# A second mixer's seven-product gate: one product's weight tiles split later, and forms of x made in fewer steps with copies on another queue

## The chip, the core and the metric

The kernel runs on one core of a Trainium2 chip. The core has TensorE (PE, matrix products; its weight loads are listed as PEld), VectorE (DVE), ScalarE (ACT), GpSimd (POOL) and SyncE (SP), each with its own queue of instructions that it works through in order; DMA transfers are issued from such queues, here from those of SP and POOL. Engines wait for one another by semaphores. The metric is the time of one execution in microseconds on the device; lower is better.

## The reference

A decoder trunk of two layers for an input of 512 positions and width 1024, all in fp32. Each layer adds a token mixer and then a gated convolutional feed-forward block, each followed by a layer norm:

```python
for i in range(DEPTH):                       # DEPTH = 2
    y = gla_mixer(...) if i % 3 == 0 else gdn_mixer(...)
    h = layer_norm(ALPHA * h + y, ...)
    h = layer_norm(ALPHA * h + conv_ffn(h, ...), ...)
```

The second mixer, which the change is about, is a gated DeltaNet with 8 heads of 128 and chunks of 64:

```python
proj = x @ w_in
qkv, gate, beta_lin, a_lin = jnp.split(proj, [...])
qkv = silu(causal_dwconv(qkv, conv_w))
o = rms_norm(gdn_chunked(qc, kc, vc, beta, gc), norm_w)
return (o * silu(gate)) @ w_out
```

`gdn_chunked` solves one unit lower triangular system per head and chunk, and then carries a state from chunk to chunk. `gate` is the product of x with a 1024 by 1024 part of `w_in`.

## The kernel before

Every fp32 product is made as three products of rounded halves (fp32r): x is kept as xh + xl, and each weight tile, 128 x 1024 in fp32, is split into wh and wl: ACT casts the tile to wh, DVE subtracts wh from the tile to get wl (`split_out`, L718). TensorE then adds wh·xh, wl·xh and wh·xl in PSUM (`mm`, L214; transposes L232).

The mixers are at 0 to 215 us (gated linear attention) and 565 to 865 us (gated DeltaNet), with the feed-forward blocks behind each.

**The seven products.** The gate's projection is made by `gated` (L1255) from seven products of half the size instead of eight, in the order of GATED: b21, b11, t1, b22, t2, t3, t4. Each has two weight tiles (i = 0 and 2) and a form of x: a quarter of x as it is (a12, a11, a22) or a sum of quarters (w1, v4, v2, v3). The third product t1 takes weights b11 + b12: after the tile of b11 is split, an accumulating DMA on POOL's queue adds the quarter b12 to the same tile in SBUF (L465, tiles `gw`). When that has landed, the tile is split again for t1, and further accumulates follow for later products. In the trace the products are the groups fold<-wh,xh, fold<-wl,xh and fold<-wh,xl; `sg` is the gate that they end in.

**When a tile is split.** `self.look` is how many tiles `prefetch` (L471) splits ahead of the one that TensorE takes; four pairs wh, wl exist (WB). `gated` sets it to 3, and to 2 in the middle of t3. The order in each engine's queue is fixed when the kernel is built, from the order of the program and a planned time for each instruction; on the chip an engine keeps to it, so a split that was planned early stands ahead of what comes behind it, whether its tile has landed or not.

**Forms of x.** `x_forms_within` (L1208) is a generator that runs beside the products: `yield n` hands back until some n us of the planned time have passed, and `until` waits for a mark. It forms w1 first; then `whole` (L1219) fills four tiles `xq` with x's quarters c and d: copies of xh by DMA, and accumulates of xl on top, all on POOL's queue. Sums and differences on DVE (L1176) make v4, v2 and v3 of them, and `put` (L1213) splits each and writes it over a quarter of xh and xl that is no longer needed (L718, xh<-xq and xl<-xq).

**What runs beside.** In the second mixer two more generators feed the engines in the same stretch: `inverses` (L1825) builds the triangular inverses in quarter and half steps (matmuls V and R, copies to T, V and rm on ACT and DVE: L1857 to L1863 for quarters, L1880 and L1883 for halves), and `chain` (L1935) carries the state for two groups of four heads: ks, vn, kT, qs, s, o on TensorE; ACT scales vn (L1960), kd (L1967) and v (L1973), and DVE makes yy (L1952), copies or updates the state (L1980, L1983) and copies o (L1989). vn needs rm, s needs vn and kd, the next ks needs the state. `mixer_out` (L1587) transposes the gated output (yT) and splits it (yh, L1145).

Of the kernel before, what the change touches and what calls it, by code (L numbers as in the profile page):

```python
# [8 lines left out]
F32 = mybir.dt.float32  # L9
# [4 lines left out]
ALU = mybir.AluOpType  # L14
# [63 lines left out]
class Trunk:  # L78
# [1129 lines left out]
    def x_forms_within(self, forms, part, pair, full, both):  # L1208


        nc = self.nc

        def put(name, ts, odd, tok):  # L1213
            for k, t in enumerate(ts):
                self.split_out(part(self.xh, odd, tok, k), part(self.xl, odd, tok, k), pair(t))
            forms[name] = (odd, tok)
            self.set(("form", name), 2.0)

        def whole(odd, tok):  # L1219
            ts = [self.slot("xq") for _ in range(2)]  # L1220
            for x, op in ((self.xh, ALU.bypass), (self.xl, ALU.add)):
                for k, t in enumerate(ts):
                    nc.gpsimd.dma_start(pair(t), part(x, odd, tok, k).bitcast(F32), accum_op=op)
            return ts

        yield from self.until(("rm", 1))
        a = full(0, 256)
        yield 1.5
        b = full(1, 256)
        yield 1.5  # L1230
        both(a, b, ALU.subtract, b)
        yield 2.0
        put("w1", b, 0, 256)
        yield from self.until(("rm", 5))
        c = whole(0, 0)
        d = whole(1, 0)
        yield from self.until(("used", "a11"))
        yield 4.0
        both(c, a, ALU.subtract, a)
        yield 2.0  # L1240
        both(b, c, ALU.subtract, b)
        yield 2.0
        both(b, d, ALU.add, d)
        c = None
        yield 2.0
        put("v4", d, 1, 0)
        d = None
        yield 3.0
        put("v2", b, 0, 0)
        b = None  # L1250
        yield from self.until(("used", "w1"))
        yield 1.0
        put("v3", a, 0, 256)

    def gated(self, forms, tag, done, last):  # L1255


        nc = self.nc
        acc = [[self.psum("fold") for _ in range(2)] for _ in range(2)]
        top, high, right = ([None, None] for _ in range(3))  # L1260

        def operand(form, c, r):
            if isinstance(forms.get(form), tuple):
                odd, tok = forms[form]
                chunk, tok = 2 * c + odd, tok + r * P
                return self.xh[:, chunk, tok:tok + P], self.xl[:, chunk, tok:tok + P]
            if form in forms:
                cols = slice(c % 2 * 256 + r * P, c % 2 * 256 + r * P + P)
                return tuple(t[:, cols] for t in forms[form][c // 2])
            chunk = 2 * c + (form != "a11")  # L1270
            tok = r * P + (256 if form == "a22" else 0)
            return self.xh[:, chunk, tok:tok + P], self.xl[:, chunk, tok:tok + P]

        def copied(ps):
            t = self.slot(tag)
            nc.scalar.copy(t, ps)
            return t

        def update(name, r):
            p, x = acc[0][r], acc[1][r]  # L1280
            if name == "b21":
                top[r] = copied(x)
            elif name == "b11":
                nc.vector.tensor_add(top[r], top[r], p)
                done(r, 1, top[r], top[r])
            elif name == "t1":
                high[r] = copied(x)
            elif name == "b22":
                right[r] = copied(x)
            elif name == "t2":  # L1290
                nc.vector.tensor_sub(right[r], right[r], p)
                done(r, 0, right[r], right[r])
            elif name == "t3":
                self.third = nc.vector.tensor_sub(high[r], high[r], p)
                self.after = None, self.third
                done(2 + r, 0, high[r], high[r])
            elif name == "t4":
                done(2 + r, 1, self.slot(tag), p)

        self.look = 3  # L1300
        for name, form, at in GATED:
            if form[0] in "vw":
                self.wait(("form", form))
            def terms(i, w, r):
                for j in range(2):
                    begin = name in ("b11", "b21", "t1") and i + j == 0
                    self.tm_terms(acc[at][r], *operand(form, i + j, r), *w[j], begin, i + j == 3, True)
                if i:
                    update(name, r)

            if name in ("t1", "t2", "t3"):
                w = [self.weight() for _ in range(2)]
                for r in range(2):
                    for i in (0, 2):
                        if name == "t3" and r and i:
                            self.look = 2
                        terms(i, w[i // 2], r)
                        if name != "t3" or not r:
                            self.pump()
                        if r:  # L1320
                            self.spend()
            else:
                for i in (0, 2):
                    w = self.weight()
                    if name == "t4":
                        self.after = ()
                    for r in range(2):
                        terms(i, w, r)
                        self.pump()
                    self.spend()  # L1330
            self.set(("used", form))
            if last:
                forms.pop(form, None)
        self.look = LOOKAHEAD
# [299 lines left out]
    def gdn(self, li, g, b):  # L1634
        nc = self.nc
# [11 lines left out]
        q, k, v, am, rm, pj = ([None] * DH for _ in range(6))  # L1647
# [284 lines left out]
        sg = [[None, None] for _ in range(NTB)]  # L1932
# [111 lines left out]
                self.spawn(finish(hf, half))  # L2044
        forms = {"apart": False}
        self.spawn(self.x_forms(forms))
        self.gated(forms, "sg", gate_done, True)
        self.wait(("r2", 1))
        self.unspill(spilled)
        self.mixer_out(y, li, g, b)  # L2050
# [76 lines left out]
```

## Time and profile before

| what | value |
|---|---|
| time, median of 3 runs | 1225.42 us (1224.86 to 1225.78) |
| the profiled execution's own time | 1226.22 us |
| its span | 1224.4 us |
| mean granted clock | 0.997 |
| ACT busy | 628.6 us (51%) |
| POOL busy | 179.5 us (15%) |
| moved by DMA | 154.65 MB |

Rows of single instructions read: start in us from the span's start, duration, engine, line, operation, out<-in, shapes, how many in a row; in brackets the idle time of the engine before it and what ended that. Tiles go by their names without numbers.

### The profile page before, as it was taken

What the parts mean: (1) busy time and instruction counts of PE and PEld (TensorE: products, weight loads), DVE (VectorE), ACT (ScalarE), POOL (GpSimd) and SP (SyncE); (2) the same over time, 40 slices, a digit from 0 to 9 for tenths busy, and PEclk for the clock granted to TensorE, in tenths of its full rate; (3) what the DMA queues carried; (4) which work ended last, traced back from release to release, by engine and by line L of the source; (5) the groups of instructions that cost most, each with busy time, mean ns of one, the idle gap of its engine ahead of it and who ended that gap; (6) DMA issues with size and microseconds to landing.
All of it is one profiled execution on the core that took longest, in us unless ns stands there. A gap on an engine that the chain in (4) does not pass through costs nothing.

```text
span 1224.4 us, 17226 instructions
## 1 busy us (share of the span) xinstructions
PE 1212.0 (99%) x6477; PEld 1023.0 (84%) x6477; DVE 923.6 (75%) x1523; ACT 628.6 (51%) x1116; POOL 179.5 (15%) x219
## 2 busy tenths in 40 slices
PE   9999999999999999999999998999999999999998
PEld 8888888988888888889888887987988888888886
DVE  6989787787767775766789966798697756775667
ACT  5666664544434443554677655873644434443440
POOL 3031101601100110001342044200520100020000
PEclk9999999999999999999999998999999999999999
DMA  8484652536733544423435259445443853393321
GB/s 233 113 165 112 135 157 67 189 104 137 196 113 104 121 93 129 128 82 105 127 108 145 82 127 155 107 149 146 131 137 97 170 180 90 99 188 89 108 65 69
DMA packets 179315, 154.65 MB, mean 126 GB/s; under 512 B 17094, under 2 KB 142090, under 8 KB 179232
## 3 DMA queue, kind: packets, MB, share of 16 engines
q1 hardware_dynamic: 161920, 115.23, 31.9%
q0 software_dynamic: 16352, 37.67, 16.1%
q8 instruction: 51, 0.84, 0.3%
q10 hardware_dynamic: 960, 0.66, 0.2%
q14 instruction: 32, 0.26, 0.1%
HBM read 133.06 MB, written 5.78 MB: 113 GB/s over the span
## 4 chain that ended last, share of the span: by engine, by line
PE 94%; DMA 2%; DVE 2%; ACT 1%; issue 0%; SPq 0%; DVEq 0%; POOL 0%; ACTq 0%; POOLq 0%
PE fm L214 54%; PE fold L214 21%; PE tm L214 11%; PE o L214 1%; PE xT L232 1%; DMA gw<-in_gdn_w_in_dram 1%; DVE wl L718 1%; PE pg L214 1%; PE yT L232 1%; DMA raw<-in_ffn_w_in_dram 0%; DMA xq<-xl 0%; PE ds L214 0%; PE V L214 0%; DMA xq<-xh 0%; PE warm L800 0%
## 5 line engine op out<-in xcount | busy, mean ns | idle before, releaser
L214 PE MATMUL fm<-xh,wh 128*128 128x512 f32 (+2 forms) x1096 | 400.4, 368 | 0.7 <-ACT xh L718 0.7
L214 PE MATMUL fm<-xl,wh 128*128 128x512 f32 (+2 forms) x1096 | 398.6, 366 | 0.0
L214 PE MATMUL fm<-xh,wl 128*128 128x512 f32 (+1 forms) x1072 | 391.4, 367 | 0.0
L718 DVE TENSOR_TENSOR wl<-raw,wh 128x1024 fp32r<-128x1024 f32 (+1 forms) x156 | 195.2, 1253 | 140.7 <-ACT wh L718 140.6
L718 ACT CAST wh<-raw 128x1024 fp32r<-128x1024 f32 (+1 forms) x157 | 162.5, 1036 | 205.6 <-PE fm L214 129.9
L214 PEld LDWEIGHTS fm<-xh,wh 128*128 128x128 f32 (+1 forms) x1096 | 205.4, 188 | 34.0 <-ACT xh L718 0.9
L214 PEld LDWEIGHTS fm<-xl,wh 128*128 128x128 f32 (+1 forms) x1096 | 205.4, 188 | 33.2 <-DVE xl L915 0.2
L214 PEld LDWEIGHTS fm<-xh,wl 128*128 128x128 f32 x1072 | 201.2, 189 | 33.1
L1021 DVE SCALAR_TENSOR_TENSOR conv<-fm,ffn_cw,conv 128x511 f32<-128x511 f32 x112 | 83.5, 746 | 9.7 <-ACT conv L1019 7.8
L718 ACT CAST wh<-b 128x1024 fp32r<-128x1024 f32 x48 | 50.2, 1053 | 74.0 <-PE fold L214 34.0
L214 PE MATMUL fold<-wh,fh 128*128 128x512 f32 x224 | 87.6, 391 | 0.0
L214 PE MATMUL fold<-wl,fh 128*128 128x512 f32 x224 | 87.3, 390 | 0.0
L214 PE MATMUL fold<-wh,fl 128*128 128x512 f32 x224 | 87.2, 389 | 0.0
L718 DVE TENSOR_TENSOR wl<-b,wh 128x1024 fp32r<-128x1024 f32 x48 | 58.4, 1223 | 22.4 <-ACT wh L718 22.0
L413 POOL DMA_DIRECT2D b<-b x24 | 20.8, 914 | 354.6 <-DVE wl L718 217.6
L1039 ACT ACTIVATE conv<-conv 128x512 f32<-128x512 f32 x44 | 27.7, 630 | 66.0 <-DVE conv L1021 66.0
L1629 DVE SCALAR_TENSOR_TENSOR conv<-fm,gdn_cw,conv 128x511 f32<-128x511 f32 (+2 forms) x72 | 54.1, 789 | 8.1 <-ACT conv L1627 7.5
L214 PEld LDWEIGHTS fold<-wh,fh 128*128 128x128 f32 x224 | 42.0, 188 | 9.7 <-DVE h L1110 1.0
L214 PEld LDWEIGHTS fold<-wh,fl 128*128 128x128 f32 x224 | 42.1, 188 | 8.8
L214 PEld LDWEIGHTS fold<-wl,fh 128*128 128x128 f32 x224 | 42.1, 188 | 8.7
L1021 DVE SCALAR_TENSOR_TENSOR form<-fm,ffn_cw,form 128x511 f32<-128x511 f32 x64 | 47.7, 746 | 1.1
L931 POOL TENSOR_TENSOR h<-h,gb 128x512 f32<-128x512 f32 x16 | 24.9, 1575 | 135.7 <-PE xT L232 134.3
(364 smaller groups left out, 2070.5 us busy)
## 6 DMA issues: line engine op xcount, KB each, us to landing
raw<-in_ffn_w_in_dram SPq DMA_DIRECT2D x88, 512.0 KB, 3.9
raw<-in_gdn_w_in_dram SPq DMA_DIRECT2D x28, 512.0 KB, 4.1
b<-in_ffn_w_out_dram SPq DMA_DIRECT2D x24, 512.0 KB, 5.9
b<-b POOLq DMA_DIRECT2D x24, 512.0 KB, 4.7
raw<-in_ffn_w_out_dram SPq DMA_DIRECT2D x20, 512.0 KB, 3.7
raw<-in_gla_w_in_dram SPq DMA_DIRECT2D x18, 512.0 KB, 4.1
gw<-in_gla_w_in_dram POOLq DMA_DIRECT2D x8, 512.0 KB, 7.1
raw<-in_gla_w_out_dram SPq DMA_DIRECT2D x8, 512.0 KB, 3.6
```

Source lines behind the costliest of these rows:

```text
L214: t = self.nc.tensor.matmul(out, a, b, start=start, stop=stop, skip_group_check=joined)
L232: t = self.nc.tensor.transpose(out, a, self.ident[:n, :n])
L413: self.nc.gpsimd.dma_start(out, group[src, i][:, cols], accum_op=ALU.add)
L718: return self.nc.scalar.copy(dst_h, src), self.nc.vector.tensor_sub(dst_l, src, dst_h)
L931: nc.gpsimd.tensor_mul(h[hf], h[hf], gb[hf])
L1021: nc.vector.scalar_tensor_tensor(a[:, d:], ps[:, :S - d], tap(2 - d), a[:, d:], ALU.mult, ALU.add)
L1039: nc.scalar.activation(a, a, AF.Gelu)
L1629: self.conv = nc.vector.scalar_tensor_tensor(a[:, d:], ps[:, :S - d], tap(3 - d), a[:, d:], ALU.mult, ALU.add)
```

## The change

It has four parts.

1. The second mixer calls `gated` with `spare=("b21", "b11")`: in these products `self.look` is 1, and 2 for the last tile of b11, so the tiles of t1 are split later in program order.
2. `self.look` is now set for each product. It was set to 3 once, and to 2 in t3 for all that followed; now t4 has 3 again, in both calls of the first mixer and in the second mixer.
3. In `whole` the copies of xh are issued on SP's queue (`nc.sync`); the accumulates of xl stay on POOL's.
4. In `x_forms_within` v4 is formed and written before c − a is made, and three of the pauses are gone.

```diff
--- before.py
+++ after.py
@@ -1218,9 +1218,9 @@
 
         def whole(odd, tok):
             ts = [self.slot("xq") for _ in range(2)]
-            for x, op in ((self.xh, ALU.bypass), (self.xl, ALU.add)):
+            for x, queue, op in ((self.xh, nc.sync, ALU.bypass), (self.xl, nc.gpsimd, ALU.add)):
                 for k, t in enumerate(ts):
-                    nc.gpsimd.dma_start(pair(t), part(x, odd, tok, k).bitcast(F32), accum_op=op)
+                    queue.dma_start(pair(t), part(x, odd, tok, k).bitcast(F32), accum_op=op)
             return ts
 
         yield from self.until(("rm", 1))
@@ -1235,24 +1235,20 @@
         c = whole(0, 0)
         d = whole(1, 0)
         yield from self.until(("used", "a11"))
-        yield 4.0
+        yield 5.0
+        both(b, c, ALU.subtract, b)
+        both(b, d, ALU.add, d)
+        put("v4", d, 1, 0)
+        yield 3.0
         both(c, a, ALU.subtract, a)
-        yield 2.0
-        both(b, c, ALU.subtract, b)
-        yield 2.0
-        both(b, d, ALU.add, d)
-        c = None
-        yield 2.0
-        put("v4", d, 1, 0)
-        d = None
-        yield 3.0
+        c = d = None
         put("v2", b, 0, 0)
         b = None
         yield from self.until(("used", "w1"))
         yield 1.0
         put("v3", a, 0, 256)
 
-    def gated(self, forms, tag, done, last):
+    def gated(self, forms, tag, done, last, spare=()):
 
 
         nc = self.nc
@@ -1297,8 +1293,8 @@
             elif name == "t4":
                 done(2 + r, 1, self.slot(tag), p)
 
-        self.look = 3
         for name, form, at in GATED:
+            self.look = 1 if name in spare else 3
             if form[0] in "vw":
                 self.wait(("form", form))
             def terms(i, w, r):
@@ -1327,6 +1323,8 @@
                     for r in range(2):
                         terms(i, w, r)
                         self.pump()
+                    if i and name == "b11" and spare:
+                        self.look = 2
                     self.spend()
             self.set(("used", form))
             if last:
@@ -2044,7 +2042,7 @@
                 self.spawn(finish(hf, half))
         forms = {"apart": False}
         self.spawn(self.x_forms(forms))
-        self.gated(forms, "sg", gate_done, True)
+        self.gated(forms, "sg", gate_done, True, ("b21", "b11"))
         self.wait(("r2", 1))
         self.unspill(spilled)
         self.mixer_out(y, li, g, b)
```

Lines behind the change move up by 2 to 4 (L1860 is L1858, L1883 is L1881, L1967 is L1965, L1980 is L1978). No engine gets another instruction; four DMAs move from POOL's queue to SP's.

**Place 1: the split of t1's tiles, ACT.** At the end of product b21 and in b11; `wh_6751` and `wh_6824` are t1's two tiles before, `wh_6898` and `wh_6991` after; T and V are copies of the inverses. Before:

```order
L1276 COPY sg_6764<-fold_6620 128x512
L718 CAST wh_6751<-gw_6459 128x1024
L1860 COPY T_6379<-R_6766 32x8x32
L718 CAST wh_6824<-gw_6471 128x1024
L1880 COPY V_6538<-V_6837 64x512
L1276 COPY sg_6807<-fold_6621 128x512
L718 CAST wh_6912<-raw_6756 128x1024
```

After:

```order
L1272 COPY sg_6752<-fold_6620 128x512
L1858 COPY T_6379<-R_6754 32x8x32
L718 CAST wh_6898<-gw_6459 128x1024
L718 CAST xh<-xq_6785 128x2x256
L1878 COPY V_6538<-V_6823 64x512
L1272 COPY sg_6795<-fold_6621 128x512
L718 CAST wh_6991<-gw_6471 128x1024
L718 CAST wh_6998<-raw_6903 128x1024
```

The copy of T stands ahead of the first cast now, and the copy of V ahead of the second; a cast of a form (xh<-xq) has come between.

The same place on DVE, where rm is what vn on TensorE reads. Before (`wl_6752` and `wl_6825` are t1's):

```order
L718 TENSOR_TENSOR wl_6752<-gw_6459,wh_6751 128x1024
L1863 COPY rm_6381<-R_6766 32x4x32
L1863 COPY rm_6383<-R_6766 32x4x32
L1907 TENSOR_SCALAR gd_x_6809<-gd_ssq_4886 128x32
L718 TENSOR_TENSOR wl_6825<-gw_6471,wh_6824 128x1024
L1163 TENSOR_TENSOR xq_6798<-xh,xl 128x512
L732 TENSOR_SCALAR gd_rr_4887<-gd_x_6809 128x32
L1883 COPY rm_6253<-R_6838 64x4x64
L733 TENSOR_SCALAR gd_rr_4887<-gd_rr_4887 128x32
L734 TENSOR_SCALAR gd_x_6809<-gd_x_6809 128x32
L1883 COPY rm_6255<-R_6838 64x4x64
```

After (`wl_6899` is t1's first tile):

```order
L1861 COPY rm_6383<-R_6755 32x4x32
L1163 TENSOR_TENSOR xq_6785<-xh,xl 128x512
L732 TENSOR_SCALAR gd_rr_4887<-gd_x_6797 128x32
L1176 TENSOR_TENSOR xq_6785<-xq_6737,xq_6785 128x512
L733 TENSOR_SCALAR gd_rr_4887<-gd_rr_4887 128x32
L734 TENSOR_SCALAR gd_x_6797<-gd_x_6797 128x32
L718 TENSOR_TENSOR wl_6899<-gw_6459,wh_6898 128x1024
L1163 TENSOR_TENSOR xq_6786<-xh,xl 128x512
L736 TENSOR_TENSOR rs_t_1060_6799<-gd_rr_4887,gd_x_6797 128x32
L1881 COPY rm_6253<-R_6824 64x4x64
L737 TENSOR_TENSOR rs_t_1060_6799<-rs_t_1060_6799,gd_rr_4887 128x32
L1881 COPY rm_6255<-R_6824 64x4x64
```

The two copies rm_6253 and rm_6255 of a half step stood behind both splits and stand behind the first now. Some rows earlier on DVE, where the tiles of b11 are split (`wl_6623`, `wl_6628` before, `wl_6742`, `wl_6813` after), the rows were:

```order
L1163 TENSOR_TENSOR xq_6747<-xh,xl 128x512
L718 TENSOR_TENSOR wl_6623<-gw_6459,wh_6622 128x1024
L1883 COPY rm_6199<-R_6697 64x4x64
L718 TENSOR_TENSOR wl_6628<-gw_6471,wh_6627 128x1024
L1883 COPY rm_6201<-R_6697 64x4x64
```

and are:

```order
L1163 TENSOR_TENSOR xq_6737<-xh,xl 128x512
L1881 COPY rm_6199<-R_6687 64x4x64
L1881 COPY rm_6201<-R_6687 64x4x64
L1163 TENSOR_TENSOR xq_6738<-xh,xl 128x512
L718 TENSOR_TENSOR wl_6742<-gw_6459,wh_6741 128x1024
L1766 TENSOR_TENSOR dt_5310<-dt_5310,pq_6725 128x512
L1766 TENSOR_TENSOR dt_5312<-dt_5312,pq_6731 128x512
L1905 TENSOR_SCALAR gd_x_6797<-gd_ssq_4886 128x32
L718 TENSOR_TENSOR wl_6813<-gw_6471,wh_6812 128x1024
```

The two rm copies and one more step to w1 stand ahead of b11's first split now.

**Place 2: the forms and the chain, DVE.** `state_6982` before and `state_6970` after are the state of the second group of heads; `xq_6952` to `xq_6959` before and `xq_6940` to `xq_6947` after are the tiles that `whole` fills. Before:

```order
L1176 TENSOR_TENSOR xq_6747<-xq_6952,xq_6747 128x512
L1176 TENSOR_TENSOR xq_6797<-xq_6797,xq_6952 128x512
L1176 TENSOR_TENSOR xq_6748<-xq_6953,xq_6748 128x512
L1176 TENSOR_TENSOR xq_6798<-xq_6798,xq_6953 128x512
L1176 TENSOR_TENSOR xq_6958<-xq_6797,xq_6958 128x512
L1980 COPY state_6982<-s_7043 128x512
L1989 COPY v_6010<-o_7049 128x512
L1176 TENSOR_TENSOR xq_6959<-xq_6798,xq_6959 128x512
L718 TENSOR_TENSOR xl<-xq_6958,xh 128x2x256
```

After:

```order
L1176 TENSOR_TENSOR xq_6785<-xq_6785,xq_6940 128x512
L1176 TENSOR_TENSOR xq_6737<-xq_6940,xq_6737 128x512
L1176 TENSOR_TENSOR xq_6786<-xq_6786,xq_6941 128x512
L1176 TENSOR_TENSOR xq_6946<-xq_6785,xq_6946 128x512
L1176 TENSOR_TENSOR xq_6947<-xq_6786,xq_6947 128x512
L1176 TENSOR_TENSOR xq_6738<-xq_6941,xq_6738 128x512
L718 TENSOR_TENSOR xl<-xq_6785,xh 128x2x256
L1978 COPY state_6970<-s_7043 128x512
L1987 COPY v_6010<-o_7049 128x512
```

The state's copy stands behind six steps on forms and a split, where it stood behind five steps. On ACT, before:

```order
L1960 ACTIVATE vn_6988<-vn_6983,gd_bp_4883 128x128 x4
L1967 ACTIVATE kd_6994<-kT_6993,gd_ebl_4880 128x128 x4
L1960 ACTIVATE vn_7019<-vn_7014,gd_bp_4883 128x128 x4
L1973 ACTIVATE v_5797<-qs_7034,gd_eb_4878 128x128
L1967 ACTIVATE kd_7025<-kT_7024,gd_ebl_4880 128x128 x4
L1973 ACTIVATE v_5797<-qs_7034,gd_eb_4878 128x128 x3
L718 CAST xh<-xq_6958 128x2x256
```

and after:

```order
L1958 ACTIVATE vn_6976<-vn_6971,gd_bp_4883 128x128 x4
L718 CAST xh<-xq_6785 128x2x256
L1965 ACTIVATE kd_6982<-kT_6981,gd_ebl_4880 128x128 x4
L1958 ACTIVATE vn_7019<-vn_7014,gd_bp_4883 128x128 x4
L1971 ACTIVATE v_5797<-qs_7034,gd_eb_4878 128x128
L1965 ACTIVATE kd_7025<-kT_7024,gd_ebl_4880 128x128 x4
L1971 ACTIVATE v_5797<-qs_7034,gd_eb_4878 128x128 x3
L718 CAST xh<-xq_6946 128x2x256
```

A cast of v2's first half (xq_6785 less xq_6940, written over a quarter of xh) has come in ahead of kd.

**Place 3: the copies of x, POOL and SP.** POOL before:

```order
L465 DMA gw_6459<-in_gdn_w_in_dram 128x2x512
L465 DMA gw_6471<-in_gdn_w_in_dram 128x2x512
L465 DMA raw_6756<-in_gdn_w_in_dram 128x2x512
L1223 DMA xq_6952<-xh 128x2x256
L1223 DMA xq_6953<-xh 128x2x256
L1223 DMA xq_6958<-xh 128x2x256
L1223 DMA xq_6959<-xh 128x2x256
L1223 DMA xq_6952<-xl 128x2x256
L1223 DMA xq_6953<-xl 128x2x256
L1223 DMA xq_6958<-xl 128x2x256
L1223 DMA xq_6959<-xl 128x2x256
```

POOL after:

```order
L465 DMA gw_6459<-in_gdn_w_in_dram 128x2x512
L465 DMA gw_6471<-in_gdn_w_in_dram 128x2x512
L465 DMA raw_6903<-in_gdn_w_in_dram 128x2x512
L1223 DMA xq_6940<-xl 128x2x256
L1223 DMA xq_6941<-xl 128x2x256
L1223 DMA xq_6946<-xl 128x2x256
L1223 DMA xq_6947<-xl 128x2x256
```

and SP after:

```order
L327 DMA raw_7518<-in_gdn_w_out_dram 128x2x512
L1223 DMA xq_6940<-xh 128x2x256
L1223 DMA xq_6941<-xh 128x2x256
L1223 DMA xq_6946<-xh 128x2x256
L1223 DMA xq_6947<-xh 128x2x256
L327 DMA raw_7532<-in_gdn_w_out_dram 128x2x512
```

The copies of xh are gone from POOL's queue and stand on SP's between two loads of output weights.

## The prediction

> **What bounds the kernel now.** I read the page's busy times and chain first, then what TensorE waits for, then a table of five-microsecond windows around the one place where it waits, then single rows there.
>
> ```profile
> span 1224.4 us, 17226 instructions
> PE 1212.0 (99%) x6477; PEld 1023.0 (84%) x6477; DVE 923.6 (75%) x1523; ACT 628.6 (51%) x1116; POOL 179.5 (15%) x219
> PE 94%; DMA 2%; DVE 2%; ACT 1%; issue 0%; SPq 0%; DVEq 0%; POOL 0%; ACTq 0%; POOLq 0%
> ```
>
> TensorE is busy 1212.0 of 1224.4 us, so all its idle time is 12.4 us. The change alters no matmul, so it can gain only from that idle time and from time at a lower clock.
>
> ```profile
> PE vn L214 <- DVE rm L1883: 4.7, 1, 4.7
> PE warm L800 <- POOL one L103: 1.0, 1, 1.0
> 740.00:745.00 5.00, 0.34 (x4) 0.15 (x2) 3.06 (x11) 3.15 (x4) 2.04 (x2) 0.85 0.55 67
> 745.00:750.00 5.00, 5.00 (x43) 4.36 (x44) 4.05 (x13) 3.22 (x10) 2.03 (x4) 0.50 1.00 149
> 750.00:755.00 5.00, 5.00 (x42) 4.41 (x41) 4.24 (x10) 2.54 (x11) 2.43 (x4) 0.97 0.99 211
> ```
>
> The first two lines are waits of TensorE (total, times, longest), the others windows: after the length come the busy times of PE, weight load, DVE, ACT and POOL, then the granted clock and the DMA share. There is one large wait, 4.7 us in the second mixer, and the window behind it runs at a granted clock of 0.50.
>
> ```profile
> 739.64 0.60 PE L214 MATMUL vn<-v,rm 128*128 128x128 f32 x4
> 744.91 0.80 PE L214 MATMUL vn<-v,rm 128*128 128x128 f32 x2 [4.66 <-DVE rm L1883]
> 749.41 0.63 PE L214 MATMUL fold<-wl,xh 128*128 128x512 f32 x1
> 749.84 0.61 PE L214 MATMUL fold<-wh,xl 128*128 128x512 f32 x1
> 750.27 0.42 PE L214 MATMUL fold<-wh,xh 128*128 128x512 f32 x1
> 750.52 0.39 PE L214 MATMUL fold<-wl,xh 128*128 128x512 f32 x1
> ```
>
> Folds follow each other by 0.43 us before 750.27 and by 0.25 behind it. From 744.91 to 750.27 are 5.36 us; at twice the speed they would be 2.7 shorter. The place is thus worth 4.66 + 2.7 = 7.4 us, and no other reachable place is worth one.
>
> **The later split.** Why vector copies hold up TensorE is seen in the rows ahead of that wait.
>
> ```profile
> 731.16 1.25 POOL L465 DMA_DIRECT2D gw<-in_gdn_w_in_dram  x1 [14.22 <-DVE wl L718]
> 732.75 1.20 POOL L465 DMA_DIRECT2D gw<-in_gdn_w_in_dram  x1 [0.34 <-DVE wl L718]
> 737.81 1.05 ACT L718 CAST wh<-gw 128x1024 fp32r<-128x1024 f32 x1 [3.60 <-DMA gw<-in_gdn_w_in_dram]
> 738.88 0.36 ACT L1860 COPY T<-R 32x256 f32<-32x256 f32 x1
> 741.54 1.04 ACT L718 CAST wh<-gw 128x1024 fp32r<-128x1024 f32 x1 [2.30 <-DMA gw<-in_gdn_w_in_dram]
> 729.65 1.22 DVE L718 TENSOR_TENSOR wl<-gw,wh 128x1024 fp32r<-128x1024 f32 x1
> 730.90 0.42 DVE L1883 COPY rm<-R 64x256 f32<-64x256 f32 x1
> 731.24 1.21 DVE L718 TENSOR_TENSOR wl<-gw,wh 128x1024 fp32r<-128x1024 f32 x1
> 738.89 1.23 DVE L718 TENSOR_TENSOR wl<-gw,wh 128x1024 fp32r<-128x1024 f32 x1 [3.07 <-ACT wh L718]
> 742.62 1.23 DVE L718 TENSOR_TENSOR wl<-gw,wh 128x1024 fp32r<-128x1024 f32 x1 [1.91 <-ACT wh L718]
> 743.76 0.69 DVE L1163 TENSOR_TENSOR xq<-xh,xl 128x512 f32<-128x512 f32 x1
> 744.45 0.41 DVE L1883 COPY rm<-R 64x256 f32<-64x256 f32 x1
> ```
>
> The two accumulating transfers that make the third product's tiles land 6.65 and 8.79 us after issue (737.81 − 731.16, 741.54 − 732.75), 3.73 apart. ACT's cast and DVE's subtraction of both tiles stand ahead of the copies into rm. So the wait ends with the second landing.
>
> In the changed order only the first tile's split stands ahead of those copies. But its transfer is issued later: two rm copies (0.34 each from start to start, 731.24 − 730.90) and one xq step (0.69, 744.45 − 743.76) now go ahead of the subtraction that releases it. It starts 1.37 later than 729.65 and ends at 732.24; the issue follows 0.29 behind, as before (731.16 − 729.65 − 1.22), and the landing 6.65 later at 739.2. Cast (1.05, to 740.2), subtraction (1.23, to 741.4), one xq step (0.69) and the rm copy (0.41) follow: 742.5 instead of 744.9. **This takes 2.4 us off the wait**, which leaves 2.3 behind 740.24 (739.64 + 0.60).
>
> Whether 2.3 us idle also halves the clock no row of this size shows: the nearest are 4.66, which was followed by 0.50, and the 1.0 of the table. The loss lies between 0 and 2.7; I take 0, since less than half of that wait remains. **The half clock gives 2.7 back.** The Trainium skill, page "TensorE: Matmul & The Clock Gate", section "Why this matters for your kernels", says the same in a rule, no idle gaps over some 3 us; by it 2.3 leaves the clock alone and 4.66 does not, as the trace has it, and the sum is the same.
>
> **The forms of x.** The second place is where the forms v4 and v2 are made.
>
> ```profile
> 748.30 1.18 POOL L465 DMA_DIRECT2D raw<-in_gdn_w_in_dram  x1 [2.97 <-DVE rs_t L736]
> 749.19 2.51 POOL L1223 DMA_DIRECT2D xq<-xh  x3
> 756.39 4.91 POOL L1223 DMA_DIRECT2D xq<-xl  x4 [2.15 <-DMA xq<-xh]
> 760.21 1.29 DVE L1176 TENSOR_TENSOR xq<-xq,xq 128x512 f32<-128x512 f32 x2 [1.27 <-DMA xq<-xl]
> 761.83 1.29 DVE L1176 TENSOR_TENSOR xq<-xq,xq 128x512 f32<-128x512 f32 x2 [0.32 <-DMA xq<-xl]
> 764.13 0.68 DVE L1980 COPY state<-s 128x512 f32<-128x512 f32 x1
> 749.52 1.14 ACT L718 CAST xh<-xq 128x512 fp32r<-128x512 f32 x2
> 760.13 1.14 ACT L1967 ACTIVATE kd<-kT,gd_ebl 128x128 f32<-128x128 f32 x4 [1.52 <-PE vn L214]
> 761.32 1.16 PE L214 MATMUL s<-vn,kd 128*128 128x128 f32 x8
> 766.00 1.06 PE L214 MATMUL o<-vn,dt 128*128 128x128 f32 x8
> 770.00:775.00 5.00, 5.00 (x41) 4.73 (x40) 3.85 (x8) 5.00 (x17) 1.19 (x1) 1.00 0.02 3
> ```
>
> Before, the accumulates of xl waited for the copies of xh on the same queue; the first landed at 760.2, the next 1.62 behind it. TensorE ran on meanwhile: kd and s needed no form, and the copy of s to the state stood behind three landings only.
>
> The plain copies go to SyncE's queue, where their neighbours are two loads of output weights that nobody waits for yet, so their issue costs nothing. Their landing no longer sets the accumulates'; the weight accumulates ahead in POOL's queue do. The first of those is issued at 741.4 + 0.29 = 741.7, lands at 748.4, and the two behind it 3.73 apart, at 752.1 and 755.8. The first xl follows 1.6 later at 757.4, if the copies take nothing from it. They write as many bytes each as an xl accumulate: as an estimate four at half of its 1.6 are 3.2. So the first landing lies between 757.4 and 760.6; I take 758.2, near the lower end, as queues have gaps (DMA share 0.55 in 740 to 745). It comes 2.0 earlier than before.
>
> The Trainium skill, page "DMA: Bandwidth & Descriptors", section "Issuing engines are not separate DMA queues", says that transfers from all issuers run on the same 16 engines, so another queue saves only issue time. By it alone the upper end, 760.6, holds; no run here shows this mix.
>
> The new wait is in the order: the cast of v2's first half now stands ahead of kd on ACT, and six xq steps and a subtraction ahead of the state copy on DVE. The cast waits for the first landing. Behind it are queued kd, two groups of vn and kd, then all of ACT; s on TensorE waits for kd. Xq 0.65, cast 0.57 and the first kd some 0.4: s starts 1.6 after the landing, at 759.8. Without this wait TensorE would reach it at 761.32 − 2.4 − 2.7 = 756.2. **So 3.6 of the 5.1 us won are given back at s.**
>
> Then the state copy: the fourth landing (3 × 1.62 behind the first) and three steps more (0.6 each) stand ahead of it, so it starts 6.7 behind the first landing, where it had 3.9 (764.13 − 760.21). The next o that reads the state had 1.2 to spare before (766.00 − 764.13 − 0.68); now it starts as the copy ends, 7.4 behind the landing: 758.2 + 7.4 = 765.6 instead of 766.00. Of the 1.5 us still won at s (761.32 − 759.8) that leaves 0.3, so **1.2 are given back here**. Ends: nothing, where folds cover it (six of them stand ahead at 0.23), and 1.9, where ACT, full from 765 to 775, passes on the moved cast (0.57) too. From there on the same work follows, and TensorE was full.
>
> **The edit for all calls.** Setting the look-ahead in each product also makes it 3 in the seventh product of both mixers, where it was 2 from the sixth on. Five folds move ahead of transposes yT in the first mixer, and a split of an output weight ahead of one gate update on DVE.
>
> ```profile
> 150.00:160.00 10.00, 9.93 (x49) 8.06 (x48) 9.95 (x20) 7.27 (x14) 0.00 (x0) 1.00 0.17 54
> 160.00:170.00 10.00, 10.00 (x54) 8.45 (x53) 9.29 (x18) 6.95 (x15) 0.00 (x0) 1.00 0.43 139
> 805.00:815.00 10.00, 10.00 (x54) 8.36 (x53) 10.00 (x24) 7.29 (x11) 0.00 (x0) 1.00 0.19 54
> ```
>
> TensorE has 0.07 us idle to win there, and the 1.2 us split is covered by the folds moved ahead (5 × 0.23). I take 0; uncovered it costs 1.2 in each mixer.
>
> **The sum.** −2.4 − 2.7 + 3.6 + 1.2 + 0 = −0.3 against the profiled run's own 1226.22 us (span 1224.4 and 1.8 around it): 1225.9. That run lay 0.8 above the median 1225.42, so the forecast is 1225.1, no change that can be measured (0.2%, 2.45 us, is about what a measurement of this kernel can tell from none).
>
> **Rivals.** First, the forms don't bind: if the xl accumulates overtake what I have queued ahead, or are early enough to land by 754.6 (756.2 − 1.6), s does not wait and the whole 5.1 stay: 1220.3; with the first wait gone wholly too, 1218.0. For it: the accumulates are issued some 7 us earlier than 756.39. Against it: the three weight accumulates ahead of them. A landing in between leaves 1222.
>
> Second, and slower: the wait at s is itself long enough to halve the clock. 3.6 us lies between the 1.0 that left no trace and the 4.66 that did. With the landing at the upper end (760.6) the o that reads the state starts at 768.0, 2.0 later than before, the moved cast adds 0.6 in the full ACT, and the half clock costs up to 2.7, of which the waits for the next landings hide most: I count 0.8. That is +3.4: 1228.8. It decides from a landing behind 759.7, where the sum passes 2.45. By the page on the clock gate named above a gap over some 3 us does this each time; the only such gap in this trace, 4.66, agrees, and by that rule the half clock's 0.8 belongs in the forecast too (1225.9).
>
> Third, the change doesn't do what it says: the rm copies still stand behind the first split. If that tile lands at 741.5, as the second did, the 4.66 remain, the form wait is hidden in turn (s and o come no earlier than before), and the time is 1225.4.
>
> **How the numbers follow.** Forecast, within 0.2%: 0.38, and the third rival, also within, 0.07. The first rival, faster: 0.33. The second, slower: 0.18. The last 0.04 are the yT transposes, half each side. So faster 0.35, same 0.45, slower 0.20. The forecast's own range is from 1223.1 (landing 757.4, no state delay) to 1228.2 (760.6, full delay). To hold 8 in 10, the range takes in the first rival but its last end: 1219.5 to 1228.5.
>
> **What would show it.** The wait of vn on rm falls to about 2.3 us, at 740.2, with the granted clock at 1.00 behind it. A new wait of s on kd, or kd's on a cast of xh, appears near 756 to 760, of 3 to 4 us; its cast starts 0.7 behind the first landing of xl, near 758. The yT transposes near 160 and 812 show no new wait. A first wait of over 4 us, an xl landing before 755 or behind 760, or no wait at s, would each prove a step wrong.

## The result and the profile after

The changed kernel takes 1228.55 us (median of 9 runs, 1227.56 to 1229.81), the kernel before 1225.78 us beside it (9 runs). The ratio is 1.0023, with a 95% interval from 1.0013 to 1.0033: slower by 2.8 us. The profiled execution has a span of 1226.5 us, 2.1 us more than before. One of the 11 runs of the look-ahead alone, further below, was slow (2032.9 us) and is left out of its median and ratio.

The waits of TensorE in the changed kernel, as in the table shown for before (total, times, longest):

```profile
PE s L214 <- ACT kd L1965: 4.1, 1, 4.1
PE vn L214 <- DVE rm L1881: 3.2, 1, 3.2
PE warm L800 <- POOL one L103: 1.0, 1, 1.0
PE fm L214 <- ACT xh L718: 0.7, 1, 0.7
```

One wait of 4.7 us has become two, of 3.2 and 4.1. The windows around them in the changed kernel (length, busy PE, weight load, DVE, ACT, POOL, granted clock, DMA share, GB/s):

```profile
740.00:745.00 5.00, 1.75 (x11) 1.56 (x10) 3.68 (x10) 4.63 (x7) 1.18 (x1) 0.85 0.39 63
745.00:750.00 5.00, 5.00 (x53) 4.34 (x52) 4.37 (x11) 3.37 (x10) 1.32 (x2) 0.81 0.88 119
750.00:755.00 5.00, 5.00 (x45) 4.53 (x45) 4.04 (x10) 3.43 (x11) 1.04 (x1) 1.00 1.08 260
755.00:760.00 5.00, 4.52 (x34) 3.94 (x32) 1.72 (x4) 1.21 (x5) 3.63 (x3) 1.00 1.11 214
760.00:765.00 5.00, 1.42 (x8) 1.42 (x9) 2.68 (x4) 2.95 (x10) 2.42 (x2) 0.90 0.90 138
765.00:770.00 5.00, 5.00 (x31) 4.72 (x31) 4.43 (x10) 3.99 (x17) 0.00 (x0) 0.76 0.72 107
```

Each wait has a stretch of lower clock behind it. The single rows of the changed kernel show how the second one comes about:

```profile
743.72 1.23 PE L214 MATMUL vn<-v,rm 128*128 128x128 f32 x4 [3.25 <-DVE rm L1881]
753.29 1.05 PE L214 MATMUL ks<-state,conv 128*128 128x128 f32 x8
742.82 1.18 POOL L465 DMA_DIRECT2D gw<-in_gdn_w_in_dram  x1 [6.08 <-DMA gw<-in_gdn_w_in_dram]
747.04 1.19 POOL L465 DMA_DIRECT2D gw<-in_gdn_w_in_dram  x1 [3.04 <-DVE gd_rr L738]
747.48 4.37 SPq L1223 DMA_DIRECT2D xq<-xh  x4
749.86 1.18 POOL L465 DMA_DIRECT2D raw<-in_gdn_w_in_dram  x1 [1.63 <-DVE gd_rr L738]
756.02 3.63 POOL L1223 DMA_DIRECT2D xq<-xl  x3 [4.97 <-DMA xq<-xh]
761.14 2.11 DVE L1176 TENSOR_TENSOR xq<-xq,xq 128x512 f32<-128x512 f32 x3 [4.42 <-DMA xq<-xl]
761.86 0.62 ACT L718 CAST xh<-xq 128x512 fp32r<-128x512 f32 x1 [5.39 <-DVE xq L1176]
762.39 1.14 ACT L1965 ACTIVATE kd<-kT,gd_ebl 128x128 f32<-128x128 f32 x4
763.58 1.74 PE L214 MATMUL s<-vn,kd 128*128 128x128 f32 x8 [4.06 <-ACT kd L1965]
769.14 1.06 PE L214 MATMUL o<-vn,dt 128*128 128x128 f32 x8
```

Read from the bottom: s waits for kd, kd stands behind the cast of v2, the cast waits for an xq step, and that for the first landing of xl, at 761.1. Before, it had landed at 760.2. One row more matters: POOL issues the first xl only at 756.02, when a copy of xh has landed, against 756.39 before. The other queue has brought that issue forward by only 0.4 us. TensorE was ahead of before by 2.13 us at ks (753.29; before 755.42), and behind by 2.26 at s (763.58; 761.32) and by 3.14 at the next o (769.14; 766.00). At the end of the program it is 2.1 to 2.3 behind; where it catches up is only known in part: the wait of xT for a layer norm, near 855, is 0.8 before and 0.2 now.

### The profile page after: what moved, and what is told of

The parts are those of the page before. It is cut to its first block, busy times and chain, and to the rows that moved or that the text cites. A ratio compares the mean times of both kernels' runs of the same rounds, so it can differ in the third digit from the quotient of the medians.

```text
span 1226.5 us, 17239 instructions
## 1 busy us (share of the span) xinstructions
PE 1212.5 (99%) x6477; PEld 1023.4 (83%) x6477; DVE 923.8 (75%) x1523; ACT 629.0 (51%) x1116; POOL 176.4 (14%) x215
## 4 chain that ended last, share of the span: by engine, by line
PE 83%; DVE 9%; issue 3%; DMA 2%; ACT 2%; SPq 1%; POOL 0%; DVEq 0%; POOLq 0%; ACTq 0%
PE fm L214 45%; PE fold L214 20%; PE tm L214 11%; DVE conv L1627 2%; DVE wl L718 2%; PE o L214 2%; PE xT L232 1%; DMA gw<-in_gdn_w_in_dram 1%; DVE tmp L1787 1%; DVE tt L1789 1%; PE yT L232 1%; PE ds L214 0%; SPq L1809 0%; PE s L214 0%; DMA xq<-xl 0%
```

## The experiments

After the result I held this theory: **the first landing of xl pins the chain**. What is won ahead of it is waited for at it; and the change makes the landing later, by its order, not by its queue. The rivals: the copies on SP's queue, or the look-ahead itself, cost the time. Each run was timed beside the kernel before.

| run | against before, with 95% interval | median |
|---|---|---|
| the change | 1.0023 (1.0013 to 1.0033) | 1228.55 |
| change, copies on POOL | 1.0024 (1.0014 to 1.0034) | 1229.12 |
| change, old steps | 1.0010 (1.0001 to 1.0019) | 1227.27 |
| change, old look-ahead | 1.0019 (1.0010 to 1.0028) | 1228.04 |
| before, look-ahead alone | 1.0014 (1.0005 to 1.0023) | 1227.44 |
| change, DVE adds | 0.9978 (0.9969 to 0.9987) | 1223.24 |
| look-ahead alone, two buffers more | 1.0028 (1.0017 to 1.0039) | 1229.52 |
| change, two buffers more | 1.0014 (1.0005 to 1.0023) | 1227.51 |
| before, two buffers more | 0.9995 (0.9986 to 1.0003) | 1225.55 |
| change, DVE adds, steps 2.6 apart | 0.9969 (0.9957 to 0.9980) | 1222.35 |
| change, steps 2.6 apart | 1.0003 (0.9994 to 1.0012) | 1226.29 |
| before, DVE adds | 0.9986 (0.9977 to 0.9995) | 1224.46 |
| change, look-ahead of t4 at 2 | 1.0024 (1.0015 to 1.0033) | 1229.29 |

### One part undone, or one done alone

The copies back on POOL:

```diff
-            for x, queue, op in ((self.xh, nc.sync, ALU.bypass), (self.xl, nc.gpsimd, ALU.add)):
+            for x, queue, op in ((self.xh, nc.gpsimd, ALU.bypass), (self.xl, nc.gpsimd, ALU.add)):
```

> The change with its third part undone: the copies of xh are back on POOL's queue; look-ahead and steps as in the change. In the built order the cast of v2's first half now stands behind kd on ACT; the six steps and the split still stand ahead of the state copy on DVE. Theory (the order of the forms costs, the queue of the copies does not): the first landing of xl stays within 1 us of the change's 761.1; the wait of s on kd (4.06) is gone or below 1, a wait for the state comes later; 1225 to 1227. Rival (the copies on SP's queue slow the weight accumulates and everything behind): the xl landings come 2 us or more earlier and the time falls to 1222 to 1224.

1229.12 us, above the expected range. The landing stayed where the theory had it, at 761.94, and the rival's early landing did not come. The wait at s is gone, but 4.0 us came at o in two waits, 3.2 in the first, since vn now stands behind the cast. The waits of this run, and its first step on a form:

```profile
PE o L214 <- ACT vn L1958: 4.0, 2, 3.2
PE vn L214 <- DVE rm L1881: 3.5, 1, 3.5
...
761.94 1.29 DVE L1176 TENSOR_TENSOR xq<-xq,xq 128x512 f32<-128x512 f32 x2 [4.89 <-DMA xq<-xl]
```

The old steps and pauses:

```diff
-        yield 5.0
-        both(b, c, ALU.subtract, b)
-        both(b, d, ALU.add, d)
-        put("v4", d, 1, 0)
-        yield 3.0
-        both(c, a, ALU.subtract, a)
+        yield 4.0
+        both(c, a, ALU.subtract, a)
+        yield 2.0
+        both(b, c, ALU.subtract, b)
...
```

> The change with its fourth part undone: the old order of steps and pauses for the forms; look-ahead and copies on SP's queue as in the change. The cast stands behind kd again and the state copy behind six steps without the split. Theory (the order of the forms costs): the wait of s on kd is gone; 1224 to 1226.5. Rival (the copies' queue costs): the time stays at 1228 to 1229 with another wait of 3 to 4 us near 760 to 766.

1227.27 us, between the two expected ranges: s no longer waits, but o waits 2.1 us for vn. The landing is at 761.6 here too.

The old look-ahead:

```diff
+        self.look = 3
         for name, form, at in GATED:
-            self.look = 1 if name in spare else 3
...
-        self.gated(forms, "sg", gate_done, True, ("b21", "b11"))
+        self.gated(forms, "sg", gate_done, True)
```

> The change with its first and second parts undone: the look-ahead is 3, and 2 from t3 on, as before; copies on SP's queue and new steps stay. Theory: the wait of vn on rm is 4.7 us again with half clock behind it; TensorE then comes to s 2 us later and waits less there, 1.5 to 3 us; together 1228 to 1231, no better than the change. Rival (the look-ahead is what costs): 1225 to 1226.

1228.04 us, as the theory had it, with a smaller wait: 4.4 us at rm, then 1.2 at s and 1.1 for the state copy, with the first landing at 759.0. So the forms cost something even when TensorE comes late, and even when the landing is 1.2 earlier than in the kernel before.

The kernel before with the look-ahead alone (both other parts undone, so the diff is those of the first two runs together):

> The kernel before with the change's look-ahead alone (first and second parts). Theory: the wait of vn on rm is 3.2 us as in the change, s does not wait for a cast, the state copy stands behind five steps as before; the landings of xl are not earlier than 760, so part of what the first wait gave is lost at the state: 1223 to 1225.5. Rival (the look-ahead itself costs): 1227 or more.

1227.44 us: here the rival's number came, and my theory's did not. The rows of this run show why, and correct the theory. Its wait, its first landing and the vn that o waits for:

```profile
PE o L214 <- ACT vn L1962: 3.7, 1, 3.7
...
761.64 1.29 DVE L1176 TENSOR_TENSOR xq<-xq,xq 128x512 f32<-128x512 f32 x2 [4.88 <-DMA xq<-xl]
763.02 1.14 ACT L1962 ACTIVATE vn<-vn,gd_bp 128x128 f32<-128x128 f32 x4 [3.94 <-DVE xq L1176]
764.21 1.22 PE L214 MATMUL o<-vn,dt 128*128 128x128 f32 x4 [3.70 <-ACT vn L1962]
```

No form stands ahead of this vn on ACT, yet it waits for a step on a form. In the built program it gets the buffer of c's first tile, and so must wait until the last step that reads this tile is done (761.64 + 1.29), which waits for the landing. The same pair stands in the kernel before, with an idle time too small to notice:

```profile
761.54 1.14 ACT L1960 ACTIVATE vn<-vn,gd_bp 128x128 f32<-128x128 f32 x4 [0.28 <-DVE xq L1176]
762.73 1.16 PE L214 MATMUL o<-vn,dt 128*128 128x128 f32 x8 [0.26 <-ACT vn L1960]
```

With 4.7 us lost earlier, TensorE came just as the first xl had landed. So the landing pinned the kernel before already, and among the waits of TensorE these 0.26 us were the only sign of it. And the landing moves with the look-ahead: it is at 761.1 to 761.9 in the four kernels so far that have the new one, and at 759.0 and 760.2 with the old. The first weight accumulate behind those of t1 is issued at 742.8 to 743.1 with the new one, and at 739.8 and 740.4 with the old. So the later split that lets TensorE come earlier also lets the forms come later.

### The pin taken away

The quarters c and d by DVE additions, as a and b are made, so no transfer is waited for:

```diff
-        c = whole(0, 0)
-        d = whole(1, 0)
+        c = full(0, 0)
+        d = full(1, 0)
```

> The change with c and d made by additions on DVE (as a and b are) instead of the copies and accumulates by DMA, so nothing of the forms waits for a landing. Theory (the first landing of xl pins the chain, through the buffers and queues of the forms): vn still waits for rm some 3.2 us, no wait over 1 us follows before 780, 1220.5 to 1223. Rival (the look-ahead or the new order of steps costs by itself): 1226 or more.

1223.24 us, 5.3 less than the change, 0.2 beside the range; the first wait is 3.3. The windows of this run where the change waits:

```profile
755.00:760.00 5.00, 5.00 (x37) 4.51 (x36) 5.00 (x11) 2.92 (x9) 1.19 (x1) 1.00 0.16 29
760.00:765.00 5.00, 5.00 (x38) 4.56 (x38) 3.48 (x7) 4.90 (x22) 0.00 (x0) 1.00 0.73 105
765.00:770.00 5.00, 5.00 (x44) 4.87 (x43) 4.75 (x16) 5.00 (x18) 0.00 (x0) 1.00 0.02 7
```

TensorE is busy without a gap at full clock. The look-ahead and the new steps are still in, so together they cost nothing that can be seen once no landing is waited for. The edit takes the eight transfers away with the landing, so it does not tell the wait from the load that they put on the queues. The same edit in the kernel before:

> The kernel before with c and d made by additions on DVE. Theory: its wait of 4.7 us and the half clock stay, and TensorE had lost only 0.26 us to the landing, so nothing is won: 1224.5 to 1226.5. Rival (the landing cost before too, further back): 2 us or more faster.

1224.46 us, just below the theory's range and short of the rival's 2 us: 1.5 us less (28 runs of before: 1225.98), with a wait of 4.3 at rm and half clock still there. So the transfers had cost the kernel before more than the 0.26 us. The 1.2 us from here to the change with the same edit lie within the two intervals.

Two buffers more, `SLOTS = 47` instead of 45, take the shared buffer away from vn and leave the program's transfers as they are:

> The kernel before with the change's look-ahead alone, and 47 buffers of 128 x 512 instead of 45, so that vn of the second step no longer takes the buffer of c that an xl accumulate fills. Theory (this buffer passes the landing on to TensorE): the wait of o on vn, 3.7 us in the look-ahead alone, is gone; the state copy still stands behind the steps, so 1 to 3 us of wait come there; 1225 to 1227. Rival (the buffer does not matter): the 3.7 us and 1227.7 stay.

> The change with 47 buffers instead of 45. Theory: in the built order the cast of v2 has left its place ahead of kd, so the wait of s on kd (4.06) is gone; the state copy stays behind six steps; 1225 to 1227.5. Rival: 1228 to 1229 as the change.

> The kernel before with 47 buffers instead of 45. Theory: the only thing gone is the 0.26 us of o waiting for vn, since with the 4.7 us at rm TensorE comes there just as the first xl lands; within 1 us of before. Rival (the buffers cost before too): 2 us faster or more.

The first gave 1229.52, outside both ranges. The wait of o on vn is gone, as the theory had it, and vn is done at 757.6, ahead of the first landing at 762.4. But the state, which got c's buffer in its place, is copied on DVE behind the steps on the forms, and the next ks waits for it:

```profile
768.05 0.68 DVE L1982 COPY state<-s 128x512 f32<-128x512 f32 x1
768.79 2.07 PE L214 MATMUL ks<-state,conv 128*128 128x128 f32 x8 [6.09 <-DVE state L1982]
```

Other tiles got other buffers too, and the third accumulate was issued 3.4 us later (746.2). The second, 1227.51, at the upper end of its range, has no long wait but five of 1.0 to 1.6 us between 741 and 778. The third, 1225.55, is the same as before, as expected; o no longer waits for vn near 762, but a later o waits 1.0 at 777. These three change too much at once to weigh the buffer alone. Together with the look-ahead alone they show two ways from the landing to TensorE: the buffer of vn, and the state's place on DVE.

### The first wait, and t4

The steps of the inverses 2.6 us of planned time apart put the rm copies ahead of t1's split:

```diff
-INV_APART = 3.2
+INV_APART = 2.6
```

> The change with c and d made by additions on DVE and the steps of the inverses 2.6 us of planned time apart instead of 3.2, which puts the rm copies ahead of the split of t1's first tile. Theory: no wait of vn on rm over 1 us and no half clock at 740 to 750, and with no landing behind it the gain stays: 3.3 us of wait and 1 to 2 of clock off the additions alone (1223.2), so 1218 to 1220.5. Rival (another wait takes its place in the chain, as it did in the change): 1222 or more.

> The change with the steps of the inverses 2.6 us apart, forms still by DMA. Theory (the landing of xl pins the chain): the first wait is gone, TensorE comes to the forms 4 us or more earlier and waits that much longer there, 5 us or more, with half clock; 1226 to 1230. Rival (the first wait is what the kernel pays for): 1222 to 1224.5.

With the DVE additions: 1222.35 us (6 runs), the lowest median of all and clearly faster than both kernels, but it is the rival's number, not the theory's; its interval overlaps that of the additions alone. The wait of vn on rm is gone; the next R waits 1.4 us for V on ACT, which is behind t1's cast, and the clock falls all the same. In the change: 1226.29, 2.3 less than the change. There R waits 3.0 us at the same place, so the first wait had only changed its name. o waits 2.7 for vn, which starts at 762.1, as the third step on a form ends; the first landing was at 758.2, and other work of DVE stands in between. The number is the theory's, the waits are not: neither is the first wait gone, nor are there 5 us at the forms.

The look-ahead of t4 back at 2:

```diff
-            self.look = 1 if name in spare else 3
+            if name != "t4":
+                self.look = 1 if name in spare else 3
```

> The change with the look-ahead of t4 back at 2 in all calls, as before; all else as in the change. Theory (that side effect costs nothing): 1228 to 1229. Rival (a part of the 2.8 us comes from the yT transposes of both mixers): 0.7 us faster than the change or more.

1229.29 us, 0.3 above the range: no gain, as the theory had it.

## Why the prediction was wrong

**What bounds the kernel**: the wait at rm and the half clock were read rightly, but not what stands behind them. The prediction said that before "kd and s needed no form"; it is true of these two, and vn, one step on, did need one. The wait of 0.26 us on it was left out, and it was the row that showed how little could be won. It was not the only one. The chain of work that ended last in the kernel before, followed row by row, leaves TensorE at 752.95 for the last copy of xh and its accumulate and comes back over the state copy (start in us, length, what):

```profile
752.95 0.57 issue
753.52 4.43 DMA xq<-xh
758.00 5.43 DMA xq<-xl
763.58 0.55 issue
764.13 0.68 DVE state L1980
```

The prediction showed only the shares of this chain, in which such a stretch is hidden: 94% PE, 2% DMA.

**The later split** moved the rm copies as said. The wait fell to 3.25, not 2.3: the tile landed at 740.2 instead of 739.2, as the transfer took 7.5 us (issued at 732.73, cast at 740.22) where before it took 6.65.

**The half clock** was taken to vanish. It got shorter instead. One-microsecond windows of the changed kernel:

```profile
743.00:744.00 1.00, 0.28 (x1) 0.28 (x2) 0.97 (x5) 1.00 (x2) 1.00 (x1) 0.75 0.00 0
744.00:745.00 1.00, 1.00 (x6) 1.00 (x7) 1.00 (x5) 0.90 (x2) 0.00 (x0) 0.50 0.38 35
...
746.00:747.00 1.00, 1.00 (x24) 1.00 (x24) 0.84 (x2) 1.00 (x5) 0.00 (x0) 0.54 0.80 141
747.00:748.00 1.00, 1.00 (x17) 0.85 (x14) 0.52 (x3) 0.73 (x2) 0.96 (x1) 1.00 1.09 201
```

Half clock now ends at 746.9, where it ended at 750.3 before. From vn to ks are 9.57 us (743.72 to 753.29) against 10.51 before, so 0.9 of the 2.7 us came back. With the 1.2 of the earlier start, 2.1 were won ahead of the forms, not 5.1.

**The forms of x** is the step that failed. The landing was forecast at 758.2, came at 761.1, and lay behind the upper end, 760.6. s, which waits for it, was forecast at 759.8 and came at 763.58; 2.9 of these 3.8 us are the landing. Two sentences of the prediction were wrong.

"Queues have gaps", and so four copies that cost the landing 0.8 us of a possible 3.2, is the first. 1.1 us of the 2.9 are the accumulates ahead, issued from 742.8 instead of 741.7. The rest is the copies. The last weight accumulate ahead, issued at 749.86, and a copy issued at about the same time (us from issue to landing behind the size):

```profile
raw<-in_gdn_w_in_dram POOLq DMA_DIRECT2D x1, 512.0 KB, 9.7
xq<-xh SPq DMA_DIRECT2D x1, 256.0 KB, 8.3
```

The same accumulate took 6.3 us before. It landed at 759.6, and the first xl 1.6 behind it at 761.1, as the forecast had its place in the queue.

"Their landing no longer sets the accumulates'" is the second. An xl is added onto the copy of xh, so its issue waits for that copy to land, on whatever queue it went: the first copy was issued at 747.48 and took 7.9 us, and the first xl was issued at 756.02. The 7 us that the first rival counted on came to 0.4. Before, and in the two runs with the copies on POOL's queue and the new look-ahead, the first xl took 3.8 us from issue to landing; by that, as an estimate, it could not have landed ahead of 759.8 here, 1.6 behind the forecast, even with nothing ahead of it in the queue. In the change with the copies on POOL the weight accumulate had landed at 757.2, and the late copies alone put the landing at 761.9.

The upper end, which the Trainium skill's page "DMA: Bandwidth & Descriptors" (section "Issuing engines are not separate DMA queues") gave, came nearer than the forecast, 0.5 us short. The traces agree with this rule of the Trainium skill: the other queue brought the landing forward by 0.8 us (761.1 against 761.9), no more than the change differs from its twin with the look-ahead of t4 at 2, where it landed at 760.25.

**The new wait at s** was right: 4.06 us where 3.6 were forecast, with the clock down behind it. s starts 2.4 behind the landing, not 1.6: it waited for all four kd (1.14 us), where the first alone was counted (0.4). **The state copy** cost another 0.9 up to the next o (3.14 − 2.26), where 1.2 were forecast, half clock included. **The edit for all calls** cost nothing, as said.

Put together with the measured sizes: −2.1 ahead of the forms, +4.4 at s (from 2.13 ahead to 2.26 behind), +0.9 at the state, −0.8 behind it, where the shorter wait of xT accounts for 0.6: some +2.3, and the span is 2.1 longer. The second rival is what happened, with its landing behind 759.7 and its half clock. That its number, 1228.8, is so near is partly luck: it had o 2.0 us late without the half clock, and 2.8 with it, where o was 3.14 late, and it counted 0.6 more in ACT where 0.8 was caught up. Its chance of 0.18 was too low: the first wait, the half clock and the landing were all forecast better than they came.

What stays open is the share of each part. They don't add up: the look-ahead alone costs 1.6 us, the other two parts alone 2.2, all three 2.8, and most of these intervals overlap. And what the shared buffer costs by itself is not shown: with more buffers the state took the place of vn.

## What to carry to other kernels

Before taking out a wait, look for the next thing that arrives at its own time, here a transfer, and ask how much earlier the engine may come before it has to wait for that; a wait of 0.3 us that looks like nothing may say that the answer is "not at all", and the chain that ended last, read row by row, names the transfer. Buffers that are handed on count as queues: an instruction that uses no result of a transfer can still wait for it through the buffer. If a transfer stands on that path and an engine has time there, make the data on the engine: four additions of 0.6 us on DVE did more here than any order of the copies that was tried.

## What the hardware showed unexpectedly

The length of a wait did not decide the clock alone. In the fastest run, R waits only 1.4 us at 741.97, and its windows at one microsecond show the clock down from 743.4 to 746.8, while TensorE is busy:

```profile
741.00:742.00 1.00, 0.03 (x2) 0.03 (x2) 1.00 (x2) 0.90 (x2) 0.00 (x0) 1.00 0.81 147
743.00:744.00 1.00, 1.00 (x5) 0.82 (x4) 0.00 (x0) 1.00 (x2) 0.46 (x1) 0.72 0.00 0
744.00:745.00 1.00, 1.00 (x3) 0.75 (x3) 0.54 (x1) 0.97 (x4) 0.00 (x0) 0.50 0.85 68
```

A wait of 2.1 us in the run with the old steps was followed by 0.50 as well (766 to 767), and in the change with two buffers more waits of 1.6 and 1.2 us were followed by 1.00 throughout. Where the clock drops at the first place, the drop begins between 742.9 and 745.3, up to a microsecond and a half before TensorE resumes or as much behind it, and lasts about 3.4 us, or twice that in the kernel before, in the two kernels made from it without its look-ahead changed, and in the change with the old steps. That agrees with a window of some 3.4 us that runs by itself, as the Trainium skill's page "TensorE: Matmul & The Clock Gate" describes it (section "What's actually happening"). The bound of some 3 us for idle gaps, from the section "Why this matters for your kernels" of the same page of the Trainium skill, is no safe bound here: gaps of 1.4 and 2.1 us were followed by half clock.
